# Experts in an order made on the chip, and S5's first tiles ahead of the convolution

## The chip, the cores and the metric

The kernel runs on one core of a Trainium2 chip. The core has TensorE (PE, matrix products into PSUM), VectorE (DVE), ScalarE (ACT), GpSimd (POOL) and SyncE (SP, which issues most DMAs here). Each engine works through its own instructions in order and waits on semaphores for the others. The metric is the device time in microseconds of one execution.

## The reference

A decoder trunk of two layers over 256 tokens of width 1024, all float32. Each layer has a mixer, a feed-forward part and a gated input embedding, each followed by a layer norm.

```
z = x @ w_in ; q, kv, gates, conv input, s5 input = split(z)
o_nsa  = attention: 8 query heads, 2 kv heads; compressed blocks (a small MLP over
         windows of 32 tokens), selected blocks and a sliding window, merged by gates
o_conv = GLU, causal depthwise convolution of width 31, layer norm, swish (256 channels)
o_s5   = 16 groups of 16 channels, each drives 64 complex states; scan over the tokens
x = LN(alpha * x + concat(o_nsa, o_conv, o_s5) @ w_out)
x = LN(alpha * x + ffn(x))     layer 0: dense SwiGLU, 2816 wide
                               layer 1: top 2 of 8 experts, SwiGLU, 3584 wide
x = LN(alpha * x + sigmoid(x Wg + bg) * (p @ Wp))
```

## The kernel before

The kernel is written with a tile framework: the program allocates tiles from pools (a tag has a number of buffers), the framework inserts the semaphores and orders each engine's instructions by program order and readiness as it reckons it when the program is built. `issue_after(i)` orders instructions of a block behind `i` on the same engine. Generators (`advance(gen, n)` runs n pieces) let the program interleave the parts of a mixer.

**The mixer** (`mixer`, once for each layer). With a PSUM pool of two double banks (`acc`) and four single banks (`tr`) it projects x: first the convolution's and S5's columns, then k and v with the convolution's replication pieces in between (`conv_taps`, tiles `rep` and `cu`), then q (tiles `qa`, two token halves). Then come, in program order: the rest of `conv_taps` (64 small matmuls for each of two channel halves, tile `cps`, with the taps from a 1 MiB load), the second piece of `compress` (four 1 MiB loads of `cmp_w1` and the hidden matmul `cmph`, L835, 64 entries in the trace), the rotary embedding of q (`rope`, tiles `rm` and `qr`), its transposes (`qTp`, L719) and those of k (`kTp`, copied by L728 and L729). All of these use the `tr` banks. Loads go through a ring of four `raw` buffers, so a load waits until the buffer four loads back is free.

Then `rest` opens a second PSUM pool (three banks `s`, one each of `o`, `y`, `bu`, two `tr`) and steps through the generators in an order written out by hand, `SEQ[l]`: `a` is one item of attention (scores L924 and L926, maximum L928, exponential L932, transposes L944, output L948), `s` one of S5's eight tiles (4 for each channel half), `c` a piece of the compressed branch, `v` the convolution's norm, `w` the splitting of a piece of w_out into high and low parts (L571, L573). An S5 tile (`s5_layer`, L1023 to L1047) is a pair of small matmuls into bank `bu` (L1026), two products with the table E on VectorE (L1031, L1032), a sum and a difference (L1033, L1034), two scans (L1038), a product for the real part (L1041, on VectorE or, for the tiles in `POOLA[l]`: 4 in layer 0, 0 to 4 in layer 1, on GpSimd), and one for the imaginary part on GpSimd (L1042). Its matmuls stand behind q's last matmul and its products behind the rotary embedding (`self.order`). At the end `advance(cmp)` finishes the compressed branch, whose transposed probabilities (L900) close attention's output of a token half (L952).

**The experts** (`moe`, layer 1). The router's counts come from a matmul; expert e gathers its tokens into 128 slots by one-hot matmuls (two experts share a gather, `pair`). `expert` streams 42 loads of 1 MiB (14 each of w1 and w3, in chunks of up to 1024 columns, then 14 of w2), issued by SyncE into a ring that in the end has 18 buffers. On TensorE each group of two loads is in an `If` on the expert's count:

```python
with self.tc.If(n > SM) as many:
    emit(False)
with many.Else():
    emit(True)
```

With at most SM = 64 tokens the two output halves go to two row halves of PSUM, with matmuls of 64 rows. Experts run in the order 0 to 7, with fixed addresses of their weights. Ahead of expert 1 stands `overflow`, for experts with over 128 tokens (a branch that jumps over it here). After the last expert come the projection and the gate of the input embedding.

Of the kernel before, what the change touches and what calls it, by code (L numbers as in the profile page):

```python
# [15 lines left out]
P = 128  # L16
D = 1024
S = 256
# [139 lines left out]

TORD = (1, 0)
ORDER = (4, 5, 0, 1, 2, 3, 6, 7)  # L160
SEQ = ("ascawcswwwwacwcwasasssaavsaswwwaaa", "accawwswcscawwsawsasasvsawaaswawaw")

POOLW = (0, 2, 4, 6)
POOLN = ((6, 7, 8, 9), (4, 9, 10, 11))
# [6 lines left out]
GRP = 2  # L171
SM = 64
OVF = 1
BK = 33

KCV = (1, 2)
# [28 lines left out]
class Trunk:  # L205
# [388 lines left out]
    def mixer(self, l, mp):  # L594
# [109 lines left out]
        for ku in range(2):  # L704
# [3 lines left out]
                    qlast = self.mm3(qa[tt], xh[:, k, tk(tt)], xl[:, k, tk(tt)], wh, wl, k == 0, k == 7)  # L708
            if ku == 0:
                advance(cmp, 1)  # L710
        advance(cv)
        advance(cmp, 1)
        qT = mp.tile([P, 4, S], F32, tag="qT", name="qT")
        for tt in range(TT):
            qr = mp.tile([P, 4, 2, 64], F32, tag="pT", name="qr", bufs=2)
            rlast = rope(qr.rearrange("p g v d -> p v g d"), qa[tt].rearrange("p (v g d) -> p v g d", v=2, g=4), tt, 2, 4)
            ps = self.tr("qTp")
            for g in range(4):
                nc.tensor.transpose(ps[:, g * P : (g + 1) * P], qr[:, g].rearrange("p v d -> p (v d)"), self.ident)  # L719
            qcopy = nc.scalar.activation(qT[:, :, tk(tt)], ps.rearrange("p (g t) -> p g t", g=4), AF.Copy, scale=0.125)  # L720


        ps = self.tr("kTp")
# [3 lines left out]
        p3 = ps.rearrange("p (b t) -> p b t", b=2)  # L727
        nc.scalar.activation(self.kTz[0:64, :, 0], p3[0:64], AF.Copy)  # L728
        nc.scalar.activation(self.kTz[64:128, :, 1], p3[64:128], AF.Copy)  # L729

        self.order = [qlast.ins, rlast.ins, qcopy]

        def rest():
            if l == 0:
# [59 lines left out]
    def compress(self, l, mp, flat, kr, vv, gt, qt):  # L794
# [28 lines left out]
                )  # L823
        yield

        ps = self.tr("cmph")
        ws = []
        for j in range(2):
            w1 = a["cmp_w1"][l, j].rearrange("(i p) f -> p i f", p=P)
            ws.append([self.load(w1[:, u * 8 : u * 8 + 8], 8, 256) for u in range(2)])  # L830
        for i in range(0, 16, 2):
            for j in range(2):
                for q in range(2):
                    r = (2 * j + q) * 32
                    mm(ps[r : r + 32, 0:256], flat[:, j, i + q].rearrange("p v n -> p (v n)"), ws[j][i // 8][:, i % 8 + q], start=(i == 0), stop=(i == 14))  # L835
# [173 lines left out]
    def s5_layer(self, l, mp, u5, mix):  # L1009
        nc = self.nc  # L1010
        col = self.col
        mag, CT, E = self.s5t
        mm = nc.tensor.matmul
        BT = col("BT", 512).rearrange("p (t k s) -> p t k s", t=2, k=2)
        glu = col("glu", 512).rearrange("p (k c) -> p k c", k=2)
        y = self.bank("y", "ya").rearrange("p (c t) -> p c t", c=2)
        self.new_xT(F32)
        for ct in range(2):
            hs = []
            for q in range(4):  # L1020
                j = 4 * ct + q
                r = slice(q * 32, q * 32 + 32)
                ps = self.bank("bu", "bu").rearrange("p (k t) -> p k t", k=2)  # L1023
                with self.tc.issue_after(self.order[0]):
                    for k in range(2):
                        mm(ps[:, k], BT[r, ct, k], u5[r, ct], start=True, stop=True)  # L1026
                eb = lambda k: E[:, k, j].unsqueeze(1).to_broadcast([P, 2, S])
                t1 = mp.tile([P, 2, S], F32, tag="s5t1", name="s5t1", bufs=2)
                t2 = mp.tile([P, 2, S], F32, tag="s5t2", name="s5t2", bufs=2)
                with self.tc.issue_after(self.order[1]):  # L1030
                    nc.vector.tensor_mul(t1, ps, eb(0))  # L1031
                    nc.vector.tensor_mul(t2, ps, eb(1))  # L1032
                nc.vector.tensor_add(t1[:, 0], t1[:, 0], t2[:, 1])  # L1033
                nc.vector.tensor_sub(t1[:, 1], t1[:, 1], t2[:, 0])  # L1034
                mb = mag[:, j : j + 1].to_broadcast([P, S])
                h = mp.tile([P, 2, S], F32, tag="s5h", name="s5h", bufs=2)
                for k in range(2):
                    nc.vector.tensor_tensor_scan(h[:, k], mb, t1[:, k], 0.0, op0=ALU.mult, op1=ALU.add)  # L1038

                ea, es = (t[:, 2 * q : 2 * q + 2] for t in (self.xh, self.xl))  # L1040
                (nc.gpsimd if j in POOLA[l] else nc.vector).tensor_tensor(ea, h, eb(0), op=ALU.mult)  # L1041
                nc.gpsimd.tensor_tensor(es, h, eb(1), op=ALU.mult)  # L1042

                hs.append(((0, ea[:, 0]), (1, es[:, 1]), (2, ea[:, 1]), (2, es[:, 0])))
                if q < 3:
                    yield

            for n in range(4):
                for q in range(4):
                    var, src = hs[q][n]  # L1050
                    mm(y[q * 32 : q * 32 + 32, ct], CT[:, var, 4 * ct + q], src, start=(n == 0), stop=(n == 3))
            yield
        z = u5
        for ct in range(2):
            nc.vector.scalar_tensor_tensor(z[:, ct], u5[:, ct], col("s5_d", 1, ct), y[:, ct], op0=ALU.mult, op1=ALU.add)
        t = mp.tile([P, 2, S], F32, tag="s5t2", name="s5g", bufs=2)
        self.gelu(t, z)
        nc.vector.scalar_tensor_tensor(z, t, 1.0, z, op0=ALU.add, op1=ALU.mult)
        ps = self.bank("bu", "glu").rearrange("p (c t) -> p c t", c=2)
        sg = mp.tile([P, 2, S], F32, tag="s5t1", name="s5sg", bufs=2)  # L1060
        for ct in range(2):
            for k in range(2):
                mm(ps[:, ct], glu[:, k, ct * P : (ct + 1) * P], z[:, k], start=(k == 0), stop=(k == 1))
            nc.scalar.activation(sg[:, ct], ps[:, ct], AF.Tanh, bias=col("s5_glu_b", 1, ct), scale=0.25)
        nc.vector.scalar_tensor_tensor(z, sg, 1.0, z, op0=ALU.add, op1=ALU.mult)
        sp = mp.tile([P, 4, S], F32R, tag="uz", name="sp")
        mix[6:8] = self.split_scaled(sp[:, 0:2], sp[:, 2:4], z, 0.25)
# [175 lines left out]
    def moe(self, l, mp):  # L1243
# [15 lines left out]
        def one_hot(e, tt):  # L1259
            Dm = Da[:, e // 2 % 2]  # L1260
            for i in range(2):
                self.dml = nc.vector.tensor_scalar(Dm[:, tt, i], slots, rank[:, tt, e + i : e + i + 1], sel[:, tt, e + i : e + i + 1], op0=ALU.is_equal, op1=ALU.mult)
            return Dm[:, tt].rearrange("p i s -> p (i s)")

        def split(tt):

# [50 lines left out]
            mm(ps[:, 0:NE], self.onesr, selr[:, tt], start=(tt == 0), stop=(tt == 1))  # L1317
        cnt = mp.tile([P, NE], F32, name="cnt")
        nc.vector.tensor_copy(cnt, ps[:, 0:NE])
        cint = mp.tile([1, 1 + NE], I32, name="cint")  # L1320
        nc.vector.tensor_copy(cint[:, 1:], cnt[0:1])
        advance(got)
# [4 lines left out]
        rank2 = mp.tile([P, TT, NE], F32, name="rank2")  # L1327
        nc.vector.tensor_scalar(cnt, cnt, float(SM), float(P - SM), op0=ALU.is_le, op1=ALU.mult)
        nc.vector.tensor_tensor(rank2, rank, cnt.unsqueeze(1).to_broadcast([P, TT, NE]), op=ALU.add)

        for tt in TORD:
            with self.after(lo):
# [10 lines left out]
            advance(self.gather(th, tl, [one_hot(e, tt) for tt in range(TT)], S, GT))  # L1343

        for e in range(NE):
            if e == OVF:

                self.flush()
                ov = self.over
                main = self.turned(ov[:2])  # L1350
                self.ring, self.nload = main, 0
                self.pre = [self.load(*s) for s in self.expert_loads(j, e)[: len(main)]]
                self.ring, self.nload = [ov] * ov[2], 0
                pre, self.pre = self.pre, []
                self.overflow(j, mp, Da[:, e // 2 % 2], cint, th, tl, rank, sel, comb, y)
                self.ring, self.pre, self.nload = main + self.ring, pre, len(main)
            Dm = Da[:, e // 2 % 2]
            es = ts(e % 2)
            De = [Dm[:, tt, e % 2] for tt in range(TT)]
            D2 = mp.tile([P, TT, P], F32, tag="D2", name="D2")  # L1360
            for tt in range(TT):
                nc.vector.tensor_scalar(D2[:, tt], slots, rank2[:, tt, e : e + 1], sel[:, tt, e : e + 1], op0=ALU.is_equal, op1=ALU.mult)
            ce = [comb[:, tt, e : e + 1] for tt in range(TT)]
            n = nc.tensor.value_load(cint[0:1, e + 1 : e + 2], min_val=0, max_val=S)
            ahead = (lambda: pair(e + 1)) if e % 2 and e + 1 != NE else None
            last = e == NE - 1
            self.expert(mp, self.expert_loads(j, e), n, self.xh[:, :, es], De, [D2[:, tt] for tt in range(TT)], ce, y, ahead, norm if last else None)
            if e == NE - 2:

                lnp = self.ln_params(l, 1, mp, "tl")  # L1370
                more = mp.tile([P, 2, D], F32R, tag="th", name="more")
                bias = self.ple_bias(l, mp.tile([P, D], F32, tag="h2", name="gb"), more[:, 0])
# [325 lines left out]
```

## Time and profile before

| what | us |
|---|---|
| median of 3 runs | 1585.9 |
| lowest and highest | 1584.85, 1587.26 |
| profiled execution, its own time | 1587.09 |
| span of its trace | 1585.3 |
| mixer, layer 0: from the first work to the attention stretch's end | 0 to 158 |
| dense layer, embedding | 185 to 420 |
| mixer, layer 1: attention stretch's end | 565 |
| experts 0 and 1 | 605 to 805 |
| experts 2 to 7 | 805 to 1534 |
| end | 1534 to 1585 |

Times of stages are from the span's start. A busy engine is not by itself the bound: in each stage one looks for the engine that is never idle, and for what the others waited for. Durations come from the one profiled execution.

### The profile page before, as it was taken

To read this page: it belongs to the slowest core of one execution; us is meant where nothing else is said; L and a number is where in the kernel's file an instruction comes from. 1 tells how busy PE (TensorE), PEld (TensorE's weight loads), DVE (VectorE), ACT (ScalarE), POOL (GpSimd) and SP (SyncE) were. 2 spreads that over 40 slices of the span, in tenths; PEclk is the share of its full clock that TensorE was granted. 3 is DMA by queue.
4 is the path that set the end of the run, shared out by engine and by line. 5 is a ranking of instruction groups with operands and counts; after the bars stand their busy time and mean duration, and the time that the engine had idled before them with its cause. 6 is when DMAs were issued, how large, how long until landed. Compare 5 with 4: busy or idle time off the path is not lost.

```text
span 1585.3 us, 16969 instructions
## 1 busy us (share of the span) xinstructions
PE 1468.0 (93%) x6654; PEld 835.4 (53%) x6655; DVE 600.4 (38%) x1023; ACT 368.6 (23%) x658; POOL 200.5 (13%) x162
## 2 busy tenths in 40 slices
PE   7987999999998798977999999999999999999887
PEld 6644788876775466422434644444644464343324
DVE  7479658646744955211211103211102110312224
ACT  5255555434444532100100001100000000101012
POOL 4625107502002511000000000000000000001000
PEclk9997999999999888999999999999999999999999
DMA  8341455553553049998999999999998889999991
GB/s 280 107 186 41 173 196 182 186 178 130 177 181 133 28 163 408 402 408 333 402 409 404 408 378 367 408 409 403 337 304 283 286 280 313 366 409 408 402 365 54
DMA packets 139916, 447.37 MB, mean 282 GB/s; under 512 B 7440, under 2 KB 19344, under 8 KB 138528
## 3 DMA queue, kind: packets, MB, share of 16 engines
q1 hardware_dynamic: 138784, 439.49, 74.6%
q0 software_dynamic: 1024, 6.35, 1.1%
q8 instruction: 79, 1.29, 0.3%
q14 instruction: 29, 0.24, 0.0%
HBM read 444.76 MB, written 1.05 MB: 281 GB/s over the span
## 4 chain that ended last, share of the span: by engine, by line
PE 45%; DMA 7%; DVE 1%; ACT 1%; issue 0%; SPq 0%; DVEq 0%; ACTq 0%
PE mgu L1476 27%; PE mo L1511 13%; DMA wraw<-in_moe_w_dram 7%; PE pg L587 2%; PE hT L1452 1%; PE xe L1401 1%; PE pp L1123 0%; PE sc L1531 0%; PE sc L1530 0%; PE DT L1494 0%; ACT ht L1457 0%; ACT hb L1483 0%; DVE mgu L1440 0%; SPq L261 0%; PE xtr L350 0%
## 5 line engine op out<-in xcount | busy, mean ns | idle before, releaser
L1476 PE MATMUL mgu<-wraw,xe 128*64 128x512 f32 (+3 forms) x2048 | 547.7, 545 | 31.4 <-DMA wraw<-in_moe_w_dram 17.8
L1476 PEld LDWEIGHTS mgu<-wraw,xe 128*64 128x64 f32 (+1 forms) x2048 | 247.5, 158 | 315.0 <-issue 269.6
L1511 PE MATMUL mo<-wraw,ht 128*64 128x512 f32 (+1 forms) x896 | 271.3, 595 | 10.2 <-DMA wraw<-in_moe_w_dram 10.2
L1511 PEld LDWEIGHTS mo<-wraw,ht 128*64 128x64 f32 (+1 forms) x896 | 101.4, 157 | 168.7 <-issue 144.1
L326 DVE TENSOR_TENSOR whl<-wraw,whl 128x1024 fp32r<-128x1024 f32 (+2 forms) x106 | 135.4, 1286 | 97.4 <-ACT whl L325 96.6
L325 ACT ACTIVATE whl<-wraw 128x1024 fp32r<-128x1024 f32 (+2 forms) x106 | 105.1, 997 | 114.6 <-PE fffn_w L322 44.6
L1484 DVE TENSOR_TENSOR hb<-hb,mgu 128x512 f32<-128x512 f32 (+1 forms) x64 | 38.1, 619 | 215.4 <-PE mgu L1476 215.1
L530 POOL DMA_DIRECT2D lnp<-in_lnp_dram x5 | 2.8, 567 | 834.8 <-ACT xe L1405 700.1
L1440 DVE MEMSET mgu<- 64x512 f32 x128 | 62.1, 485 | 118.8 <-ACT hb L1483 103.1
L1457 ACT ACTIVATE ht<-hT 128x512 f32<-128x512 f32 (+1 forms) x32 | 17.4, 544 | 371.7 <-PE hT L1452 354.6
L326 DVE TENSOR_TENSOR ot<-mo,ot 128x512 fp32r<-128x512 f32 x16 | 10.6, 688 | 240.0 <-ACT ot L325 240.0
L322 PE MATMUL fffn_w<-whl,xh 128*128 128x512 f32 (+1 forms) x192 | 71.8, 374 | 0.0
L321 PE MATMUL fffn_w<-whl,xl 128*128 128x512 f32 (+1 forms) x192 | 71.6, 373 | 0.0
L320 PE MATMUL fffn_w<-whl,xh 128*128 128x512 f32 (+1 forms) x192 | 71.6, 373 | 0.0
L1483 ACT ACTIVATE hb<-mgu 128x512 f32<-128x512 f32 (+1 forms) x64 | 32.4, 543 | 166.1 <-PE mgu L1476 163.0
L1455 DVE COPY ht<-hT 128x512 f32<-128x512 f32 (+1 forms) x32 | 20.0, 625 | 134.5 <-PE hT L1452 130.5
L325 ACT ACTIVATE ot<-mo 128x512 fp32r<-128x512 f32 x16 | 9.0, 596 | 263.7 <-PE mo L1511 263.7
L320 PEld LDWEIGHTS fffn_w<-whl,xh 128*128 128x128 f32 x192 | 36.1, 188 | 6.6
L321 PEld LDWEIGHTS fffn_w<-whl,xl 128*128 128x128 f32 x192 | 36.1, 188 | 6.5
L322 PEld LDWEIGHTS fffn_w<-whl,xh 128*128 128x128 f32 x192 | 36.1, 188 | 6.3
L1452 PEld LDWEIGHTS hT<-sqr,hb 128*128 128x128 f32 x224 | 24.8, 141 | 24.1 <-issue 18.5
L653 PE MATMUL z<-xh,whl 128*128 128x256 f32 x96 | 28.2, 294 | 8.4 <-ACT whl L325 8.4
(365 smaller groups left out, 1972.2 us busy)
## 6 DMA issues: line engine op xcount, KB each, us to landing
wraw<-in_moe_w_dram SPq DMA_DIRECT2D x336, 1024.0 KB, 16.4
wraw<-in_ffn_w_dram SPq DMA_DIRECT2D x33, 1024.0 KB, 5.1
wraw<-in_cmp_w_dram SPq DMA_DIRECT2D x8, 1024.0 KB, 5.5
wraw<-in_w_out_dram SPq DMA_DIRECT2D x8, 1024.0 KB, 10.9
wraw<-in_ple_gate_w_dram SPq DMA_DIRECT2D x8, 1024.0 KB, 10.7
wraw<-in_w_in_dram SPq DMA_DIRECT2D x8, 792.0 KB, 5.8
wraw<-in_w_in_dram SPq DMA_DIRECT2D x8, 768.0 KB, 7.5
lnp<-in_lnp_dram POOLq DMA_DIRECT2D x5, 1024.0 KB, 5.1
```

The source lines that it names most:

```text
L320: mm(dst, xh, wh, start=start, stop=False)
L321: mm(dst, xl, wh, start=False, stop=False)
L322: return mm(dst, xh, wl, start=False, stop=stop)
L325: h = self.hi = self.nc.scalar.activation(dh, src, AF.Copy)
L326: return h, (low or self.nc.vector).tensor_tensor(dl, src, dh.bitcast(F32), op=ALU.subtract)
L587: end = self.nc.tensor.matmul(at(acc, c), lh(k), parts[k][0][:, c], start=start, stop=stop)
L1440: nc.vector.memset(acc[h][rows[1 - h]], 0.0)
L1452: nc.tensor.transpose(ps[:, i * P : (i + 1) * P], hbs[h][:, i * P : (i + 1) * P], self.ident)
L1476: mm(dst, x, wk, start=k == 0, stop=k == KT - 1)
L1483: nc.scalar.activation(hb[:, :hw], accs[0][h][:, :hw], AF.Silu)
L1484: nc.vector.tensor_mul(hb[:, :hw], hb[:, :hw], accs[1][h][:, :hw])
L1511: mm(dst, x, w[:, i, h * 512 : (h + 1) * 512], start=k == 0, stop=k == NK - 1)
```

## The change

It has two parts. In both mixers, S5's first two tiles are issued ahead of the rest of `conv_taps`, with their matmuls in `tr` banks of the projection's pool; both rotary embeddings of q come ahead of them; the `y` bank is taken only after the first four tiles; `compress` has one more piece, so that its four loads stay where they were and its hidden matmul, now in a `tr` bank of the second pool, follows attention's first item (a `c` more in `SEQ`). In the experts, `take_turns`, ahead of expert 1, sorts experts 2 to 7 by their counts (ties by number) with VectorE, puts them into `TURNS` (position i gets the expert with the TURNS[i]-th largest count) and permutes the columns of ranks, selections, combination weights and counts; SyncE reads each turn's expert number into a register and forms the addresses of its 42 loads from it.

```diff
-SEQ = ("ascawcswwwwacwcwasasssaavsaswwwaaa", "accawwswcscawwsawsasasvsawaaswawaw")
+SEQ = ("acsacwcswwwwacwcwasasssaavsaswwwaaa", "acccawwswcscawwsawsasasvsawaaswawaw")
+FIX = 2
+TURNS = (0, 5, 1, 4, 3, 2)
...
-        advance(cv)
-        advance(cmp, 1)
         qT = mp.tile([P, 4, S], F32, tag="qT", name="qT")
+
+        qrs = []
         for tt in range(TT):
             qr = mp.tile([P, 4, 2, 64], F32, tag="pT", name="qr", bufs=2)
             rlast = rope(qr.rearrange("p g v d -> p v g d"), qa[tt].rearrange("p (v g d) -> p v g d", v=2, g=4), tt, 2, 4)
+            qrs.append(qr)
+        self.order = [qlast.ins, rlast.ins]
+        advance(s5, 2)
+        advance(cv)
+        advance(cmp, 1)
+        for tt in range(TT):
+            qr = qrs[tt]
             ps = self.tr("qTp")
...
-
-        self.order = [qlast.ins, rlast.ins, qcopy]
...
-        ps = self.tr("cmph")
         ws = []
         for j in range(2):
             w1 = a["cmp_w1"][l, j].rearrange("(i p) f -> p i f", p=P)
             ws.append([self.load(w1[:, u * 8 : u * 8 + 8], 8, 256) for u in range(2)])
+        yield
+        ps = self.tr("cmph")
...
-        y = self.bank("y", "ya").rearrange("p (c t) -> p c t", c=2)
+        y = None
...
-                ps = self.bank("bu", "bu").rearrange("p (k t) -> p k t", k=2)
+                ps = (self.tr("bu") if j < 2 else self.bank("bu", "bu")).rearrange("p (k t) -> p k t", k=2)
...
+            if y is None:
+                y = self.bank("y", "ya").rearrange("p (c t) -> p c t", c=2)
...
+        def column(name, e):
+
+            t, c = (tables[name], e) if e < FIX else (turned[name], e - FIX)
+            return [t[:, tt, c : c + 1] for tt in range(TT)]
+
+        def take_turns():
+
+            m = NE - FIX
+            key = mp.tile([P, NE], F32, name="tkey")
+            r = mp.tile([P, m], F32, name="trank")
+            one = mp.tile([P, m, m], F32, name="tone")
+            all = mp.tile([P, 4 * TT, m], F32, name="tall")
+            both = mp.tile([P, 4 * TT, m, m], F32, name="tboth")
+            got = mp.tile([P, 4 * TT, m], F32, name="tgot")
+            row = mp.tile([1, 2, m], I32, name="trow")
+            nc.vector.scalar_tensor_tensor(key, count, float(NE), slots[:, :NE], op0=ALU.mult, op1=ALU.subtract)
+            k = key[:, FIX:]
+            nc.vector.tensor_tensor(one, k.unsqueeze(1).to_broadcast([P, m, m]), k.unsqueeze(2).to_broadcast([P, m, m]), op=ALU.is_gt)
+            nc.vector.tensor_reduce(r, one, axis=AX.X, op=ALU.add)
+            for i, t in enumerate(TURNS):
+                nc.vector.tensor_scalar(one[:, i], r, float(t), None, op0=ALU.is_equal)
+            for i, t in enumerate((rank, sel, comb)):
+                nc.vector.tensor_copy(all[:, i * TT : (i + 1) * TT], t[:, :, FIX:])
+            nc.vector.tensor_copy(all[:, 3 * TT], count[:, FIX:])
+            nc.vector.tensor_copy(all[:, 3 * TT + 1], slots[:, FIX:NE])
+            wide = [P, 4 * TT, m, m]
+            nc.vector.tensor_tensor(both, all.unsqueeze(2).to_broadcast(wide), one.unsqueeze(1).to_broadcast(wide), op=ALU.mult)
+            nc.vector.tensor_reduce(got, both, axis=AX.X, op=ALU.add)
+            nc.vector.tensor_copy(row, got[0:1, 3 * TT :])
...
+            nc.vector.tensor_scalar(r, got[:, 3 * TT], float(SM), float(P - SM), op0=ALU.is_le, op1=ALU.mult)
+            nc.vector.tensor_tensor(turned["rank2"], turned["rank"], r.unsqueeze(1).to_broadcast([P, TT, m]), op=ALU.add)
+            return row
...
         for e in range(NE):
+            if e == 1:
+                row = take_turns()
             if e == OVF:
...
-            n = nc.tensor.value_load(cint[0:1, e + 1 : e + 2], min_val=0, max_val=S)
+            ce = column("comb", e)
+            which, own = e, cint[0:1, e + 1 : e + 2]
+            if e >= FIX:
+                own = row[0:1, 0, e - FIX : e - FIX + 1]
+                which = nc.sync.value_load(row[0:1, 1, e - FIX : e - FIX + 1], min_val=FIX, max_val=NE - 1)
+            n = nc.tensor.value_load(own, min_val=0, max_val=S)
...
-            self.expert(mp, self.expert_loads(j, e), n, self.xh[:, :, es], De, [D2[:, tt] for tt in range(TT)], ce, y, ahead, norm if last else None)
+            self.expert(mp, self.expert_loads(j, which), n, self.xh[:, :, es], De, [D2[:, tt] for tt in range(TT)], ce, y, ahead, norm if last else None)
```

## Rows read from the trace of the kernel before

**Rows 1.** The page's first part: busy us, share of the span, instructions.
```profile
PE 1468.0 (93%) x6654; PEld 835.4 (53%) x6655; DVE 600.4 (38%) x1023; ACT 368.6 (23%) x658; POOL 200.5 (13%) x162
```

**Rows 2.** Windows in both mixers: stretch, length, busy time by engine, clock, DMA.
```profile
74.00:88.00 14.00, 10.77 (x144) 6.88 (x137) 0.08 (x1) 3.48 (x7) 0.00 (x0) 1.00 0.60 222
88.00:158.00 70.00, 54.41 (x292) 31.47 (x291) 66.22 (x120) 38.65 (x100) 30.87 (x23) 0.83 0.23 84
...
481.70:497.00 15.30, 12.32 (x152) 7.53 (x145) 0.05 (x1) 4.43 (x8) 0.00 (x0) 0.89 0.62 223
497.00:565.00 68.00, 53.77 (x290) 30.64 (x289) 60.62 (x117) 38.97 (x107) 33.91 (x26) 0.82 0.15 55
```
The columns after the length are PE, PEld, DVE, ACT and POOL busy, the granted clock, the DMA share and GB/s.

**Rows 3.** Timeline of VectorE, both layers: start, us, instruction, idle before and releaser.
```profile
72.99 0.69 DVE L690 TENSOR_TENSOR qr<-rm,rm 128x512 f32<-128x512 f32 x1
87.92 0.69 DVE L928 TENSOR_REDUCE mx<-s 128x2 f32<-128x512 f32 x1 [14.24 <-PE s L926]
...
481.06 0.69 DVE L690 TENSOR_TENSOR qr<-rm,rm 128x512 f32<-128x512 f32 x1
497.11 0.69 DVE L928 TENSOR_REDUCE mx<-s 128x2 f32<-128x512 f32 x1 [15.35 <-PE s L926]
```

**Rows 4.** Timeline of TensorE: hidden matmul and first scores.
```profile
78.06 1.89 PE L835 MATMUL cmph<-wraw,flat 128*32 128x256 f32 x26
...
84.16 1.92 PE L835 MATMUL cmph<-wraw,flat 128*32 128x256 f32 x28 [2.75 <-DMA wraw<-in_cmp_w_dram]
86.56 1.12 PE L924 MATMUL s<-kTz,qT 128*128 128x512 f32 x2 [0.48 <-ACT chid L838]
...
495.32 1.56 PE L924 MATMUL s<-kTz,qT 128*128 128x512 f32 x2 [0.48 <-ACT chid L838]
```

**Rows 5.** Timeline of ScalarE: the last copy of k, both layers.
```profile
82.14 0.59 ACT L729 ACTIVATE kTz<-kTp 64x512 f32<-64x512 f32 x1
...
490.22 0.59 ACT L729 ACTIVATE kTz<-kTp 64x512 f32<-64x512 f32 x1
```

**Rows 6.** Windows for tile s5t alone: stretch, length, VectorE busy (instructions), clock, DMA.
```profile
88.00:158.00 70.00, 28.73 (x48) 0.83 0.23 84
497.00:565.00 68.00, 26.85 (x48) 0.82 0.15 55
```

**Rows 7.** Lines by form, layer 0 VectorE, then layer 1 GpSimd: S5's real part.
```profile
L1041 DVE TENSOR_TENSOR xh<-s5h,E 128x512 f32<-128x512 f32 x7 | 8.0, 1144 | 0.0
...
L1041 POOL TENSOR_TENSOR xh<-s5h,E 128x512 f32<-128x512 f32 x5 | 6.3, 1269 | 84.6 <-DVE s5h L1038 80.7 <-DVE su L933 3.8
```

**Rows 8.** Timeline of TensorE, layer 0: S5's matmuls, the compressed branch's end.
```profile
87.74 1.12 PE L1026 MATMUL bu<-u,pk 32*128 32x256 f32 x4
...
118.45 0.44 PE L900 MATMUL cpT<-sqr,pc 128*128 128x128 f32 x2
...
145.84 2.08 PE L952 MATMUL o<-pcT,VB 128*128 128x128 f32 x8
```

**Rows 9.** Windows by expert: experts 1, 4, 5, 6 and 7, as in group 2.
```profile
691.00:805.00 114.00, 90.60 (x440) 37.03 (x440) 23.51 (x46) 7.85 (x16) 0.00 (x0) 0.94 0.97 380
...
1042.00:1196.00 154.00, 152.83 (x419) 75.39 (x416) 21.68 (x40) 9.19 (x17) 0.00 (x0) 1.00 0.97 357
1196.00:1351.00 155.00, 153.64 (x440) 77.92 (x440) 21.73 (x40) 8.93 (x17) 0.60 (x1) 1.00 0.87 290
1351.00:1434.00 83.00, 81.03 (x412) 31.69 (x410) 20.11 (x38) 7.41 (x15) 1.95 (x3) 1.00 1.02 393
1434.00:1534.00 100.00, 84.80 (x406) 30.35 (x402) 18.89 (x34) 7.52 (x16) 3.40 (x2) 1.00 1.03 406
```

**Rows 10.** Timeline of VectorE: a small instruction of the router.
```profile
612.96 0.14 DVE L1328 TENSOR_SCALAR cnt<-cnt 128x8 f32<-128x8 f32 x1
```

**Rows 11.** The page's DMA issues: count, KB each, us from issue to landing.
```profile
wraw<-in_moe_w_dram SPq DMA_DIRECT2D x336, 1024.0 KB, 16.4
```

**Rows 12.** The chain that ended last: SyncE issuing one load.
```profile
734.25 0.52 SPq L261
```

More of the change, by code (lines that the diff above doesn't have):

```diff
@@ L719, in mixer @@
                 nc.tensor.transpose(ps[:, g * P : (g + 1) * P], qr[:, g].rearrange("p v d -> p (v d)"), self.ident)
[L720 removed]
+            nc.scalar.activation(qT[:, :, tk(tt)], ps.rearrange("p (g t) -> p g t", g=4), AF.Copy, scale=0.125)
         ps = self.tr("kTp")
@@ L1261, in one_hot @@
             for i in range(2):
-                self.dml = nc.vector.tensor_scalar(Dm[:, tt, i], slots, rank[:, tt, e + i : e + i + 1], sel[:, tt, e + i : e + i + 1], op0=ALU.is_equal, op1=ALU.mult)
+                r, s = (column(t, e + i)[tt] for t in ("rank", "sel"))
+                self.dml = nc.vector.tensor_scalar(Dm[:, tt, i], slots, r, s, op0=ALU.is_equal, op1=ALU.mult)
             return Dm[:, tt].rearrange("p i s -> p (i s)")
+        tables = {"rank": rank, "sel": sel, "comb": comb}
@@ new lines, in moe @@
+        turned = {}
+        def column(name, e):
[24 more added lines that the diff above has]
+            nc.vector.tensor_copy(row, got[0:1, 3 * TT :])
+            for i, n in enumerate(("rank", "sel", "comb")):
+                turned[n] = got[:, i * TT : (i + 1) * TT]
+            turned["rank2"] = mp.tile([P, TT, m], F32, name="trank2")
+            nc.vector.tensor_scalar(r, got[:, 3 * TT], float(SM), float(P - SM), op0=ALU.is_le, op1=ALU.mult)
+            nc.vector.tensor_tensor(turned["rank2"], turned["rank"], r.unsqueeze(1).to_broadcast([P, TT, m]), op=ALU.add)
+            return row
@@ L1319, in moe @@
         nc.vector.tensor_copy(cnt, ps[:, 0:NE])
+        count = mp.tile([P, NE], F32, name="count")
+        nc.vector.tensor_copy(count, cnt)
         cint = mp.tile([1, 1 + NE], I32, name="cint")
@@ L1329, in moe @@
         nc.vector.tensor_tensor(rank2, rank, cnt.unsqueeze(1).to_broadcast([P, TT, NE]), op=ALU.add)
+        tables["rank2"] = rank2
         for tt in TORD:
@@ L1361, in moe @@
             for tt in range(TT):
-                nc.vector.tensor_scalar(D2[:, tt], slots, rank2[:, tt, e : e + 1], sel[:, tt, e : e + 1], op0=ALU.is_equal, op1=ALU.mult)
-            ce = [comb[:, tt, e : e + 1] for tt in range(TT)]
-            n = nc.tensor.value_load(cint[0:1, e + 1 : e + 2], min_val=0, max_val=S)
+                nc.vector.tensor_scalar(D2[:, tt], slots, column("rank2", e)[tt], column("sel", e)[tt], op0=ALU.is_equal, op1=ALU.mult)
+            ce = column("comb", e)
[4 more added lines that the diff above has]
+            n = nc.tensor.value_load(own, min_val=0, max_val=S)
             ahead = (lambda: pair(e + 1)) if e % 2 and e + 1 != NE else None
             last = e == NE - 1
-            self.expert(mp, self.expert_loads(j, e), n, self.xh[:, :, es], De, [D2[:, tt] for tt in range(TT)], ce, y, ahead, norm if last else None)
+            self.expert(mp, self.expert_loads(j, which), n, self.xh[:, :, es], De, [D2[:, tt] for tt in range(TT)], ce, y, ahead, norm if last else None)
             if e == NE - 2:
```

## The prediction

> **What bounds the kernel now.** I read the page first. TensorE is busy for nearly all of the span and VectorE for little over a third [rows 1]; such averages hide stages with different limits, so I then asked for the busy time of each engine stage by stage. Only two kinds of stage are touched here.
>
> *The mixers.* In the long stretch of attention, S5 and convolution VectorE (DVE) is busy 66.2 of 70 us in layer 0 and 60.6 of 68 us in layer 1, while TensorE has 14 to 16 us of gaps [rows 2]: VectorE sets the end there. In the 14 to 15 us just before, VectorE does next to nothing [rows 2]. Its timeline shows why: it finishes the rotary embedding of q at 73.7 us and then has no work until attention's first scores at 87.9; in layer 1 it is 481.7 and 497.1 [rows 3]. TensorE's timeline shows what it waits for. The compressed branch's hidden matmul, begun among the convolution's matmuls, waits 2.75 us for its last weights; and the first scores come right behind the copy of that hidden tile out of PSUM, at 86.6 and 495.3 [rows 4], although q and k were in place at 82.7 and 490.8 [rows 5]. Two things to see: VectorE is idle in front of a stretch that it bounds, and that stretch opens about 4 us later than attention's own inputs would allow, held by the compressed branch.
>
> *The experts.* The stages of the trace show two kinds of expert. With more than 64 tokens ("many") one takes 154 to 155 us, PE busy throughout; with 64 or fewer ("few") 83 us, or 100 us where weights are late [rows 9]. Experts 2 to 7 are many, few, many, many, few, few by how long TensorE is busy in their stages (the stages of experts 2 and 3, 805 to 957 and 957 to 1042, repeat the two patterns and are not among the rows; experts 0 and 1 are few). Each has 42 loads of 1 MiB (336 of them for 8 experts, [rows 11]); at the 406 GB/s of the starved stage that is 2.58 us each and 108 us an expert. So a many expert lets the queue run ahead by some 46 us, a few expert uses up 25 us. The ring holds 18 buffers, so the lead can't pass 18 x 2.58 = 46 us: in the second of two many experts in a row the DMA share falls to 0.87 [rows 9].
>
> **The change, part by part.**
>
> *S5's first two tiles ahead of the convolution.* One tile on VectorE is six instructions on the s5t tiles plus the product for the real part. The six cost 28.73/8 = 3.59 us in layer 0 and 26.85/8 = 3.36 us in layer 1 [rows 6]; the product is 1.14 us on VectorE in layer 0 and is on GpSimd for these tiles in layer 1 [rows 7]. Two tiles are 9.5 and 6.7 us, together 16.2. They depend on u5, the table E and one small matmul pair each, ordered behind q's last matmul and the rotary embedding, so they may start at 73.7 and 481.7 and fit into the 14.2 and 15.4 us of idleness with 4.7 and 8.7 us to spare. In the old kernel they could not, since their PSUM bank belonged to the pool that opens when the projection's pool closes; the edit takes two of the projection's banks. Cost on TensorE: 1.1 us of matmuls a tile [rows 8], 2.2 us ahead of the convolution's last matmuls; the banks of q come free with the rotary embedding, which adds at most the 2 us by which that lags.
>
> *The compressed branch later.* Its hidden matmul now comes after attention's first item. Of its 64 entries in the trace 28 stood behind q and k; the other 36 stood in front, among the convolution's, and at 1.92/28 us each [rows 4] they give back 2.5 us. First scores then need only q and k: 82.7 + 2.2 - 2.5 = 82.4, so about 82.9 in place of 86.6 (3.7 us), and 491.0 in place of 495.3 (4.3 us). What gets late is the compressed result: its last transpose is at 118.5, its consumer, the close of attention's first output, at 145.8 [rows 8]. A delay of some 6 us of the branch lies inside those 27 us; without that cover it would cost the 6. In the same edit the weights' fourth load still waits for the taps' buffer; nothing of it is now waited for by the scores.
>
> *What of this reaches the end.* Bounds: 0, if every freed microsecond turns into another wait; 16.2 + 8.0 = 24.2, if VectorE stays as dense as it was. It will not quite, for the two tiles were filler between attention's dependent steps. Its idle share in the stretch is now 5% and 11% [rows 2]. I let it rise to 10% and 15%: layer 0 from 84.2 (the first maximum is 1.4 us behind the scores) with 66.2 - 9.5 = 56.7 us of work ends at 147.2 against 158, gain 10.8; layer 1 from 492.8 (1.8 behind) with 60.6 - 6.7 = 53.9 us ends at 556.2 against 565, gain 8.8. That is 19.6. Some 1.6 us are taken off for PSUM banks and for the hidden matmul in front of attention's second item: 18. All stages behind (the dense layer with TensorE full, and the expert loads, which start on events of the second mixer) begin earlier by the same amount.
>
> *The order of experts 2 to 7.* By counts, turns 0, 5, 1, 4, 3, 2 give many, few, many, few, few, many. Follow the lead of the loads. Both orders start the same: from 0 at expert 2 (stage 691 to 805 is bound by loads: TensorE idle 23 us at 380 GB/s [rows 9]), to about 46, down to 20, up to full again. Before: many (full, the queue is held up), then two few ones, which use 50 us against a lead of less than 46, some buffers being in use or in flight: 17 us of waiting (100 - 83) at the end. After: the two few ones stand right behind the same full ring, so they wait the same 17 us in the middle, and the many one last needs no lead. The sum is 3 x 154.5 + 3 x 83 + 17 = 730 us either way. I take 0 for the order, with bounds of -17 (the wait vanishes) and +17 (it comes twice).
>
> *Making it.* About 19 VectorE instructions, most as small as the 0.14 us one in [rows 10] and two of 288 columns: some 4 us. VectorE is busy 23.5 of 114 us in the stage of expert 1 and TensorE waits for weights there for longer than that; hidden, 0. Without that cover: 4 us. The six register reads on SyncE and the addresses made from a register are not in the trace. A plain load occupies the queue's issuer for 0.52 us out of the 2.58 us that its data take [rows 12]; below, 0; above, what a rival says. I take 0, nearest to that row.
>
> Sum: -18 - 0 - 0. The profiled execution took 1587.1 us (span 1585.3), 1.2 above the median of the runs, 1585.9; on the median the forecast is **1568 us**. A difference under 0.2% (3.2 us) can't be told from none here.
>
> **Rivals.**
>
> *The order pays too (0.07).* If the ring at the two few experts were fuller than I reckon, the wait of 17 us would be mostly gone: 1554. Against it: the same ring was full in front of them in the old order.
>
> *The freed time becomes other waits (0.12).* Attention's chain of scores, maximum, exponential, transposes may set the pace once S5 no longer fills its gaps; ScalarE is at half load, PE has gaps. Gain 0 to 6, about 1583; half of this lies within 0.2%. For it: 12 items that depend step by step. Against: VectorE's 5% idleness, which leaves no sign of waiting.
>
> *The tiles don't move (0.03).* If the two banks are not free until the rotary embedding is over and the convolution is served first, VectorE gets the work only when attention starts: 1585.
>
> *Register-addressed loads are slow (0.08, the other side).* Place: SyncE, 252 loads of experts 2 to 7. Of the two few experts' 84 loads, 66 must arrive while they run; with t us per load the time rises by 66 x (t - 2.58). At t = 2.85 this eats all 18 us; at t = 3.0 it is 28 us, 1596, slower than before. Against: a plain issue is 0.52 us, so an address would have to cost more than 2 us. [...]
>
> **How the numbers follow.** The forecast has 0.70, and its own range is 1559 to 1578. Faster by over 0.2%: 0.70 + 0.07 + 0.06 = 0.83. Within: 0.06 + 0.03 = 0.09. Slower: 0.08. The range 1556 to 1584 takes in the 24.2 us bound with some 5 us of it for the order, and most of the small gains; it leaves out the slow loads, the full 17 us of the order and the outer part of the forecast, some 0.18.
>
> **What would show it.** Right: VectorE busy with s5t instructions right after the rotary embedding in both layers; first scores about 4 us closer to the end of q; the VectorE-bound stretch ending about 11 and 9 us sooner; the last expert a many one without waits for weights, and 15 to 17 us of such waits in the two few ones before it; expert stages of 154 and 83 us. Wrong: s5t work still beside attention, a new gap in attention's first items on the hidden matmul, DMA share under 1 while TensorE waits for weights (slow loads), or no wait left in the few pair (the order pays).

## The result, and the profile after

The changed kernel takes 1568.1 us (median; 1566.98 to 1571.78), the kernel before 1585.94 on the same chip: ratio 0.9888, 95% interval 0.9876 to 0.9900. The profiled execution took 1566.98 us (span 1565.2) against 1587.09. The page's first part (answers to [rows 1]; VectorE's work is as before):

```profile
PE 1463.2 (93%) x6654; PEld 831.8 (53%) x6655; DVE 596.8 (38%) x1043; ACT 367.7 (23%) x658; POOL 200.0 (13%) x162
```

VectorE's timeline of layer 0 (columns as in [rows 3]): the first two S5 tiles fill 71.9 to 80.2 us, the first maximum comes at 81.23 in place of 87.92.

```profile
71.28 0.69 DVE L692 TENSOR_TENSOR qr<-rm,rm 128x512 f32<-128x512 f32 x1
71.89 0.68 DVE L1039 TENSOR_TENSOR s5t<-bu,E 128x512 f32<-128x512 f32 x1
...
79.49 0.69 DVE L1049 TENSOR_TENSOR xh<-s5h,E 128x512 f32<-128x512 f32 x1
81.23 0.69 DVE L936 TENSOR_REDUCE mx<-s 128x2 f32<-128x512 f32 x1 [1.05 <-PE s L934]
...
131.32 3.31 DVE L575 TENSOR_TENSOR wlo<-wraw,whi 128x512 fp32r<-128x512 f32 x2
134.56 1.74 DVE L1008 RECIPROCAL crs<-crs 128x256 f32<-128x256 f32 x1
136.22 2.18 DVE L575 TENSOR_TENSOR wlo<-wraw,whi 128x512 fp32r<-128x512 f32 x2
...
139.52 0.15 DVE L941 RECIPROCAL su<-su 128x2 f32<-128x2 f32 x1
139.60 0.67 DVE L936 TENSOR_REDUCE mx<-s 128x4 f32<-128x512 f32 x1
...
140.19 0.15 DVE L943 TENSOR_TENSOR su<-su,gt 128x2 f32<-128x2 f32 x1
```

TensorE's timeline (answers to [rows 4, 8]):

```profile
79.88 1.12 PE L932 MATMUL s<-kTz,qT 128*128 128x512 f32 x2 [1.34 <-ACT kTz L738]
...
87.56 1.05 PE L843 MATMUL cmph<-wraw,flat 128*32 128x256 f32 x10
88.54 0.66 PE L956 MATMUL o<-pT,vv 128*64 128x128 f32 x8
89.13 3.22 PE L843 MATMUL cmph<-wraw,flat 128*32 128x256 f32 x54
...
110.70 0.38 PE L908 MATMUL cpT<-sqr,pc 128*128 128x128 f32 x2
...
119.94 1.10 PE L999 MATMUL cmean<-cy,sqr 128*128 128x256 f32 x4
...
141.59 1.11 PE L952 MATMUL pT<-sqr,p 128*128 128x128 f32 x4 [9.20 <-POOL p L946]
...
145.84 0.71 PE L960 MATMUL o<-pcT,VB 128*128 128x128 f32 x4
```

The scores wait for k's copy alone; the hidden matmul stands behind them and no longer waits for a load. New is the wait of 9.2 us at 132 to 141. GpSimd is named, but it had to wait for VectorE in turn:

```profile
140.50 1.04 POOL L946 TENSOR_TENSOR p<-p,su 128x512 f32<-128x512 f32 x1 [3.26 <-DVE su L943]
```

It needs two VectorE instructions of 0.15 us on the item's sums (`su`). ScalarE had these sums ready at 126.3, but in VectorE's list above the two stand behind weight splits (`wlo`) and the convolution's norm.

The windows of the two stretches, from the first maximum to the first matmul of the output projection (answers to [rows 2]):

```profile
81.20:149.20 68.00, 54.20 (x347) 31.37 (x348) 55.08 (x108) 37.75 (x94) 27.23 (x22) 0.87 0.35 130
88.00:100.00 12.00, 12.00 (x140) 7.56 (x136) 6.69 (x20) 8.21 (x21) 2.81 (x2) 1.00 0.71 267
...
482.00:546.00 64.00, 53.15 (x340) 32.30 (x338) 52.25 (x105) 38.13 (x96) 26.74 (x22) 0.86 0.32 119
```

VectorE (DVE) has 11 us less work in layer 0 and 8 less in layer 1 (66.2 and 60.6 before; 9 less in layer 1 if the window of before, too, runs to that matmul, at 565.85), but is idle for 12.9 and 11.8 us. In 88 to 100 us TensorE is full and VectorE busy for 6.7 of 12.

The windows of experts 2 to 7 (answers to [rows 9]):

```profile
788.50:939.00 150.50, 150.07 (x408) 74.43 (x408) 21.16 (x40) 7.88 (x15) 0.00 (x0) 1.00 1.02 397
939.00:1027.00 88.00, 85.06 (x441) 37.06 (x440) 22.33 (x42) 8.93 (x19) 0.00 (x0) 1.00 1.02 395
1027.00:1178.60 151.60, 150.37 (x408) 74.42 (x408) 20.74 (x38) 8.05 (x16) 0.00 (x0) 1.00 0.97 354
1178.60:1266.50 87.90, 85.29 (x441) 35.32 (x440) 21.95 (x41) 9.01 (x19) 0.60 (x1) 1.00 1.02 395
1266.50:1363.50 97.00, 85.00 (x408) 31.11 (x408) 20.46 (x38) 7.64 (x16) 1.95 (x3) 1.00 1.03 406
1363.50:1514.00 150.50, 150.05 (x408) 74.45 (x408) 19.16 (x34) 7.87 (x15) 3.37 (x2) 1.00 0.80 316
```

Many, few, many, few, few, many; the second of the two few ones waits for weights at 406 GB/s, the last one for nothing. From TensorE's first instruction behind expert 1's last output matmul to its first behind the last expert's, the six take 725.7 us (788.47 to 1514.16) against 728.7 before (805.67 to 1534.35).

These 3 us have a visible source. The stages of the second and the fourth of the six have 33 matmuls more in the trace (441 against 408), 32 of them the gather of the next pair of experts. TensorE's groups in the fourth:

```profile
L1460 PE MATMUL xe<-Dm,th 128*128 128x256 f32 x16 | 4.2, 296 | 0.5 <-ACT hb L1542 0.5
...
L1460 PE MATMUL xe<-Dm,tl 128*128 128x256 f32 x16 | 3.9, 285 | 0.0
```

Before, the fourth was a many expert (x440 in [rows 9]), which took 155.8 us, 4.2 more than the many one ahead of it. Now it is the first of the two few ones, which wait for loads anyway: the two together take 184.9 us, against 183.7 before, and no many expert takes over 151.6.

So the profiled execution's 20.1 us are: 1.7 before the end of q's matmuls in layer 0 (the last section has their source), 8.0 and 8.2 in the mixers from there to the end of their output projections, 3.0 in experts 2 to 7, less 0.9 elsewhere.

### The profile page after: what moved, and what is told of

It is laid out like the page before. It is cut to its first block, busy times and chain, and to the rows that moved or that the text cites. A ratio compares the mean times of both kernels' runs of the same rounds, so it can differ in the third digit from the quotient of the medians.

```text
span 1565.2 us, 17518 instructions
## 1 busy us (share of the span) xinstructions
PE 1463.2 (93%) x6654; PEld 831.8 (53%) x6655; DVE 596.8 (38%) x1043; ACT 367.7 (23%) x658; POOL 200.0 (13%) x162
## 4 chain that ended last, share of the span: by engine, by line
PE 48%; DMA 4%; ACT 1%; SPq 1%; DVE 1%; issue 1%; ACTq 0%; DVEq 0%
PE mgu L1535 29%; PE mo L1570 13%; DMA wraw<-in_moe_w_dram 4%; PE pg L589 2%; PE hT L1511 1%; PE xe L1460 1%; SPq L263 1%; PE sc L1589 0%; PE sc L1590 0%; PE pp L1133 0%; PE DT L1553 0%; ACT ht L1516 0%; ACT hb L1542 0%; ACT ot L327 0%; DVE mgu L1499 0%
## 5 line engine op out<-in xcount | busy, mean ns | idle before, releaser
L328 DVE TENSOR_TENSOR ot<-mo,ot 128x512 fp32r<-128x512 f32 x16 | 10.6, 688 | 237.5 <-ACT ot L327 237.5
L324 PE MATMUL fffn_w<-whl,xh 128*128 128x512 f32 (+1 forms) x192 | 71.9, 374 | 0.0
```

What stands on the lines that cost most here:

```text
L324: return mm(dst, xh, wl, start=False, stop=stop)
L328: return h, (low or self.nc.vector).tensor_tensor(dl, src, dh.bitcast(F32), op=ALU.subtract)
```

## The experiments

Each experiment was timed in five rounds beside the kernel before. "Mixer 0" and "mixer 1" are the profiled time from the end of q's matmuls to the end of the output projection, less that of the kernel before (117.2 and 116.1 us); "experts" is that of experts 2 to 7, less 728.7. The six runs from "S5 ahead alone" to "two ahead, end as old" have the changed kernel's experts.

| run | median, us | ratio, 95% interval | mixer 0 | mixer 1 | experts |
|---|---|---|---|---|---|
| the changed kernel | 1568.1 | 0.9876 to 0.9900 | -8.0 | -8.2 | -3.0 |
| mixers alone | 1571.1 | 0.9885 to 0.9915 | -4.8 | -8.3 | -0.3 |
| order alone | 1584.89 | 0.9975 to 0.9993 | -0.2 | +1.0 | -2.2 |
| order made, old kinds | 1573.03 | 0.9891 to 0.9922 | -6.4 | -8.1 | +1.0 |
| alternating | 1554.23 | 0.9781 to 0.9808 | -6.7 | -8.1 | -16.0 |
| S5 ahead alone | 1568.71 | 0.9861 to 0.9896 | -9.3 | -6.2 | -1.4 |
| branch later alone | 1582.95 | 0.9963 to 0.9984 | -3.9 | -0.2 | -2.8 |
| one tile ahead | 1571.24 | 0.9884 to 0.9915 | -9.7 | -4.1 | -2.4 |
| three tiles ahead | 1585.25 | 0.9971 to 0.9998 | -1.5 | -1.1 | -1.5 |
| three ahead, end as changed | 1565.79 | 0.9843 to 0.9881 | -8.2 | -11.3 | -2.7 |
| two ahead, end as old | 1566.99 | 0.9849 to 0.9886 | -6.8 | -11.9 | -1.9 |
| alternating, one and three | 1550.66 | 0.9749 to 0.9790 | -7.5 | -11.5 | -15.9 |
| alternating, splits later | 1556.17 | 0.9783 to 0.9810 | -4.5 | -9.8 | -15.9 |

A mixer of the same program text varies by 3.3 us in these columns (mixer 0 of the changed kernel, mixers alone, order made, and alternating; mixer 1 by up to 1.7 with "splits later" taken in), so smaller differences in one of them prove nothing. In these four, TensorE, VectorE, ScalarE and GpSimd have their instructions of the stretch in the same order; TensorE's granted clock is not the same (1.00 or 0.83 over the same 10 us, last section).

**Mixers alone**: the experts stay 0 to 7 with fixed addresses.

```diff
-            if e == 1:
-                row = take_turns()
...
-            self.expert(mp, self.expert_loads(j, which), n, ...)
+            self.expert(mp, self.expert_loads(j, e), n, ...)
```

> Only the two mixers are changed; experts 2 to 7 run as numbered, with fixed addresses and nothing sorted. Theory (the mixers give the gain): the trace of the changed kernel is 17.2 us ahead of the old one where the experts begin, so 1569 us (1567 to 1571), ratio 0.989. Rival (the order gives the most of it): 1577 or more.

**Order alone**: the mixers of the kernel before (all mixer lines of the diff undone), experts as changed.

```diff
-        advance(s5, 2)
...
-        yield
-        ps = self.tr("cmph")
```

> Only the order of the experts is changed; the mixers are the old ones. Theory (the order moves the wait for weights of two few experts in a row from the end to the middle): no more than the 3 us by which the expert stage of the changed kernel is shorter, so 1583 to 1587. Rival (the order gives the most): 1577 or less.

**Order made, old kinds**: the order is made on the chip, and comes out as many, few, many, many, few, few.

```diff
-TURNS = (0, 5, 1, 4, 3, 2)
+TURNS = (0, 5, 1, 2, 4, 3)
```

> The whole change, but the turns are set so that kinds come as in the old order: many, few, many, many, few, few, still sorted on the chip and loaded from register addresses. Theory (making the order costs nothing): as the mixers alone, within 2 us. Rival (sorting, register reads or register addresses cost something that the order then repays): above the mixers alone by that price, 3 us or more.

**Alternating**: many, few, many, few, many, few.

```diff
-TURNS = (0, 5, 1, 4, 3, 2)
+TURNS = (0, 5, 1, 4, 2, 3)
```

> The whole change, but the last two turns change places: many, few, many, few, many, few. Theory (what waits is the second of two few experts in a row, 83 us of work against 108 us of loads, with a lead of at most 46 us): a many expert refills the lead before each few one, so the wait of about 16 us falls to 2 to 4 and the time to 1554 to 1558. Rival (the wait belongs to whatever comes last, or the lead is not refilled): 1566 or more.

These four ran on one chip, and each came out as its theory had it (mixers alone 0.1 us above its range). The mixers give 15.3 us, the order 1.5 by the medians, and making it, with addresses from registers, cannot be told from nothing (1573.03 against 1571.1, intervals nearly the same). Alternating gives 14 us more than the changed kernel. Its last three experts by windows:

```profile
1181.40:1269.30 87.90, 85.28 (x442) 35.37 (x441) 21.97 (x41) 9.04 (x18) 0.60 (x1) 1.00 1.02 395
1269.30:1420.70 151.40, 150.40 (x408) 74.40 (x408) 20.70 (x39) 7.92 (x15) 2.90 (x4) 1.00 0.98 361
1420.70:1503.90 83.20, 81.09 (x409) 31.41 (x408) 18.98 (x34) 7.80 (x16) 2.44 (x2) 1.00 1.00 388
```

The last few expert takes 83.2 us where the changed kernel's second few one took 97.0: the many one in front of it refilled the ring (361 GB/s over its 151.4 us are 54.7 MB, 10.6 more than the 42 loads of one expert).

**S5 ahead alone**: the hidden matmul goes back ahead of the first scores.

```diff
-SEQ = ("acsacwcswwwwacwcwasasssaavsaswwwaaa", "acccawwswcscawwsawsasasvsawaaswawaw")
+SEQ = ("ascawcswwwwacwcwasasssaavsaswwwaaa", "accawwswcscawwsawsasasvsawaaswawaw")
...
+        ps = self.tr("cmph")
         ws = []
...
-        yield
-        ps = self.tr("cmph")
```

> The changed kernel with the compressed branch's hidden matmul put back among the convolution's matmuls, ahead of attention's first scores; S5's two tiles stay ahead, the experts' order stays the new one. Theory (two separate gifts: 16 us of tile work taken out of the VectorE-bound stretch, and an earlier start of that stretch): only the tile work is kept; first scores are held again by the hidden tile, so 7 to 9 us of the two mixers' gain go back and the time is 1575 to 1578. Rival (one gift: the stretch starts earlier only because VectorE and TensorE are kept busy ahead of it, the place of the hidden matmul is nothing): 1568 to 1571.

**Branch later alone**: no S5 tile ahead.

```diff
-        advance(s5, 2)
...
-                ps = (self.tr("bu") if j < 2 else self.bank("bu", "bu")).rearrange("p (k t) -> p k t", k=2)
+                ps = self.bank("bu", "bu").rearrange("p (k t) -> p k t", k=2)
```

> The changed kernel without S5's two tiles ahead of the convolution (S5 takes its first tiles beside attention, as the old kernel did); the hidden matmul stays behind attention's first item. Theory of two separate gifts: first scores come 4 to 5 us closer to the end of q in each layer and the stretch still holds all of S5's work, so some 8 us of the 15 are kept: 1574 to 1578. Rival (with S5 in it the stretch is bound by VectorE's work from the end of the rotary embedding on, so that an earlier score only queues up): 1582 to 1584.

The first theory fell in both, and both times lie in the rival's range: S5 ahead alone is as fast as the whole change, the branch alone gives 4.3 us (2.5 to 5.9), and in its profile 2.3 us stand before the end of q (the clock, 1.00 in place of 0.60 from 22 to 26 us, last section, and a wait of TensorE for VectorE ahead of it, 0.6 us in place of 1.6). TensorE's timeline and the stretches' windows of S5 ahead alone:

```profile
83.86 3.49 PE L842 MATMUL cmph<-wraw,flat 128*32 128x256 f32 x28 [2.61 <-DMA wraw<-in_cmp_w_dram]
87.83 1.12 PE L931 MATMUL s<-kTz,qT 128*128 128x512 f32 x2 [0.48 <-ACT chid L845]
```

```profile
89.20:145.00 55.80, 49.06 (x276) 28.89 (x275) 53.72 (x103) 35.67 (x83) 27.34 (x20) 0.88 0.23 86
...
485.50:545.70 60.20, 48.41 (x276) 30.11 (x274) 57.74 (x105) 36.77 (x95) 25.42 (x20) 0.82 0.25 88
```

The scores come 8 us later than in the changed kernel, and the output projection begins 4.3 us earlier (144.96 against 149.24; it ends 0.8 earlier, at 177.06): VectorE is busy for 53.7 of 55.8 us, where the changed kernel needs 68.0 for 55.1. The windows of branch later alone say the same:

```profile
79.60:152.00 72.40, 58.73 (x355) 33.07 (x356) 66.73 (x120) 39.36 (x101) 31.33 (x23) 0.83 0.31 115
485.90:561.60 75.70, 61.10 (x359) 34.59 (x358) 62.45 (x120) 40.58 (x110) 33.82 (x26) 0.80 0.23 82
```

The stretches begin earlier and get longer (from 70 and, up to the same matmul, 69 us) with the same work in them to within 1 us. The start of the scores is not what sets their end.

**One tile ahead** (`advance(s5, 1)`, one `tr` bank) and **three tiles ahead** (`advance(s5, 3)`, three banks):

```diff
-        advance(s5, 2)
+        advance(s5, 1)
...
-                ps = (self.tr("bu") if j < 2 else ...
+                ps = (self.tr("bu") if j < 1 else ...
```

> One S5 tile ahead of the convolution in each layer in place of two. Theory (each tile is worth its VectorE time, 4.8 us in layer 0 and 3.4 in layer 1): 8 us slower than the changed kernel, 1574 to 1577. Rival (the first tile fills the idle time and the second only takes its place in the queue ahead of the copies that the scores need): 1568 to 1571, as the changed kernel.

> Three S5 tiles ahead of the convolution in each layer in place of two. VectorE has 0.7 to 1.2 us left between the second tile and the first maximum in layer 0. Theory (the idle time is used up; a third tile delays the first maxima by what it takes off later): within 3 us of the changed kernel, 1565 to 1571, the first maximum of layer 0 some 4 us later. Rival (attention's steps, not VectorE's work, set the pace behind, so a third tile still pays its own time): 1560 to 1564.

One tile took 1571.24 us, just above the rival's range and below the theory's. In layer 1 the gain grows with the tiles: 0.2, 4.1 and 8.2 us with none, one and two. In layer 0 the first tile already pays all (3.9, 9.7 and 8.0). Three tiles came out as neither theory had it: nearly all is lost. TensorE's timeline of that run:

```profile
137.48 2.08 PE L1073 MATMUL glu<-u,pk 128*128 128x256 f32 x4 [7.29 <-DVE u L1068]
...
143.63 1.03 PE L999 MATMUL cmean<-cy,sqr 128*128 128x256 f32 x4
...
156.11 1.22 PE L322 MATMUL wo<-whi,ch 128*128 128x512 f32 x2 [2.75 <-ACT ch L332]
```

`SEQ` counts steps: with three tiles taken ahead, each later `s` does the next tile, and S5's end (`glu`) falls ahead of the `v` of the convolution's norm. TensorE waits 7.3 us for S5's end, the convolution's mean behind it in its queue comes at 143.6 in place of 119.9, and the output projection, which begins with the convolution (`ch`), at 156. The next two runs took steps out of `SEQ`:

```diff
 three ahead, end as changed (besides advance(s5, 3)):
-SEQ = ("acsacwcswwww...", "acccawwswcsc...")
+SEQ = ("acacwcswwww...", "acccawwwcsc...")
 two ahead, end as old:
+SEQ = ("acacwcwwww...", "acccawwwccaww...")
```

> Three S5 tiles ahead, and one step of S5 taken out of the hand-written order of each mixer, so that the fourth and later tiles and S5's end stand where the changed kernel has them. Theory (the run with three tiles lost 17 us because every later step of S5 moved up one place, so that S5's end stood ahead of the convolution's normalization on the same PSUM banks and engines, and TensorE waited 7.3 us for it): the loss goes, 1563 to 1570. Rival (a third tile costs attention's first items more than it takes off later, wherever the others stand): 1577 to 1587.

> Two S5 tiles ahead as in the changed kernel, and two steps of S5 taken out of the hand-written order of each mixer, so that the other six tiles and S5's end stand where the old kernel had them. Theory (what pays is two tiles' work less in the stretch that VectorE bounds): as the changed kernel, 1565 to 1571. Rival (what pays is that all later steps of S5, its end above all, came two places earlier in the order): most of the gain goes, 1578 to 1585.

Both theories held: the loss goes, so it came from the places of S5's later steps, and the gain of two tiles does not come from these places. In layer 1 two tiles with S5's end at its old place give as much (11.9) as three (11.3), so the third is not what pays there; in layer 0 neither gains over one tile.

**Alternating, one and three**, and **alternating, splits later**:

```diff
 one and three (besides the turns of alternating, and one s less in layer 1's SEQ):
+AHEAD = (1, 3)
-        advance(s5, 2)
+        advance(s5, AHEAD[l])
 splits later (besides the turns of alternating), the end of layer 0's SEQ:
-...asssaavsaswwwaaa
+...asssaavsasawawaw
```

> The alternating order of experts (many, few, many, few, many, few), with one S5 tile ahead in layer 0 and three in layer 1 (one later step of S5 taken out of layer 1's order, so that S5's end stands there where the changed kernel has it). Theory (the two layers add up, each as it was in the runs that tried it alone: layer 0 some 1.7 us and layer 1 some 3 us better than with two tiles, both counted from the end of q): 5 us faster than the run with the alternating order alone, 1547 to 1551. Rival (these differences come from how the build arranges each whole program and don't carry over): 1552 to 1558.

> The alternating order of experts, the mixers as in the changed kernel but for the end of layer 0's order: the last three weight splits stand between attention's last three items and no longer ahead of them. Theory (TensorE's 9.2 us wait near 140 us is VectorE's: the maximum of attention's next item is queued behind the weight splits, so with the splits later it goes first): the wait goes and layer 0's output projection ends 3 to 7 us sooner, 1547 to 1551. Rival (the output projection needs the split weights right behind, so the wait only changes its place): 1552 to 1556, with TensorE waiting for the split weights.

The first is the fastest kernel of the study by its median, 1550.66 us, though its interval overlaps that of alternating alone. Layer 1's gain carried over (-11.5). Layer 0 gives -7.5 in place of -9.7, 0.8 better than the two tiles of alternating (-6.7); that is inside the scatter, so this half of the theory is not shown. In the second the rival held, 0.2 us above its range: the wait only changed its place, to S5's end though, and not to the split weights as I had it. Its waits of TensorE, 66 to 165 us (total, times, longest), then those of the run with the alternating order alone:

```profile
PE glu L1073 <- DVE u L1068: 6.4, 1, 6.4
PE pT L952 <- POOL p L946: 4.7, 3, 2.3
```

```profile
PE pT L952 <- POOL p L946: 11.6, 3, 9.2
```

VectorE has to do the same work there, whichever consumer waits for it. The theory also had the wrong instruction: not the next item's maximum, but the waiting item's own two `su` instructions came behind the splits.

## Why the prediction was right, and where it was not

- **S5's tiles, 9.5 and 6.7 us.** Right in size for two: alone they give 9.3 and 6.2, with S5's end at its old place 6.8 and 11.9. As a price for each tile it fails in layer 0, where one gives 9.7 (5.9 more than none) and a second and third nothing more.
- **First scores 3.7 and 4.3 us earlier.** They came 5.0 and 5.7 earlier, counted from the end of q; the mechanism was right, the size a little low. The compressed result came earlier and not later: its last transpose is at 110.7 (118.45 before), its consumer at 145.84 as before, so the cover held, with more room than reckoned.
- **What of this reaches the end: the step that failed.** I let VectorE's idle share rise to 10% and 15%, which left 3.4 of the 8 us of earlier scores standing (19.6 less the tiles' 16.2), and took off 1.6 for PSUM banks and the hidden matmul. The share rose to 19% and 18% (12.9 of 68.0, 11.8 of 64.0), and beside the tiles the earlier scores are worth nothing that the runs can tell: without them the time is the same. So the rival that freed time becomes other waits was true of the scores and not of the tiles. Where it went is seen in part only. TensorE is full from 80 to 100 us (busy for 20.00 of 20) with the hidden matmul and S5's matmuls, while VectorE idles 5.3 of 12 us (0.4 in the kernel before). The new wait of 9.2 us is not the place: VectorE is busy without a gap from 130 to 140 (10.00 of 10), and taking it away in "splits later" gained nothing.
- **18 us for the mixers** came out as 16.2 in them, 1.7 ahead of the end of q that I had not foreseen, and 3 in the experts (less 0.9 elsewhere). That the time is that of the forecast is in part luck: these made up for one another. The medians are 17.8 apart.
- **The order, 0.** It is 1.5 us alone by the medians (1.1 to 4.0 by its interval). The wait for weights moved from the end to the second of the two few experts, as followed from the ring's lead; it is 13.8 us there (97.0 less 83.2) and was reckoned 17. What the sum over "either way" left out is the gather of the next pair: it took 4.2 us in a many expert and now lies where loads are waited for. All eight profiles with this order are 1.4 to 3.0 us shorter in the experts, the two with the old kinds 0.3 shorter and 1.0 longer. So the stages are not 154 and 83 us, but 151 and, with the gather, 88. The bound of -17 is what the alternating order reaches (-16.0).
- **Making the order, and register addresses, 0.** VectorE makes it at 599 to 602 us, beside expert 0's matmuls, in 2.8 us where 4 were reckoned: the rows below. The new instructions of SyncE, from its instructions at the loads' line (minimum, median and longest ns), add 46 and 29 ns to a load; the rival needed 270 to eat 18 us. The loads of the starved stage ran at 406 GB/s, as before, so no cost of SyncE's new instructions shows there.

```profile
599.15 0.15 DVE L1294 SCALAR_TENSOR_TENSOR tkey<-count,sqr 128x8 f32<-128x8 f32 x1
...
601.75 0.15 DVE L1312 TENSOR_TENSOR trank<-tgot,trank 128x12 f32<-128x12 f32 x1
```

```profile
L263 SPq FUSED_REGOPS  x252: 42/46/56, 770.5 to 1450.0; - x126
L263 SPq MOVE wraw<-in_moe_w_dram x252: 29/29/38, 770.6 to 1450.2; - x126
```

What stays open: why one tile suffices in layer 0. With one tile in place of two each engine has its instructions in another order over most of the stretch, and no run held that order fixed.

## What to carry to other kernels

Work taken out of a stretch that one engine bounds was worth about its time here (two tiles, reckoned at 9.5 and 6.7 us, gave 9.3 and 6.2), though in layer 0 the first tile gave all of it. Opening that stretch earlier was worth nothing beside it (1568.1 against 1568.71 us); the same busy time over more microseconds shows this (VectorE 66.7 over 72.4 in place of 66.2 over 70). In an order written out by hand that counts steps, moving one step ahead moves every later one: look whether it has to come out of the list too, or a consumer far behind may be late, as the output projection was here (156 us in place of 149). Where loads run ahead into a ring, as here, it paid to put a stage that lets them lead in front of each one that uses up the lead (83.2 us in place of 97.0), and other work (here the gather, 4.2 us) where the loads are waited for.

## What the runs showed of the hardware that was not expected

TensorE's granted clock near the start differs between kernels whose program text there is the same. Windows of the kernel before, then of the changed kernel, then of two ahead, end as old:

```profile
18.00:22.00 4.00, 2.25 (x16) 1.85 (x15) 3.90 (x12) 3.18 (x8) 0.00 (x0) 0.97 0.90 349
22.00:26.00 4.00, 4.00 (x24) 4.00 (x23) 3.57 (x9) 0.86 (x1) 0.00 (x0) 0.60 0.84 219
```

```profile
18.00:22.00 4.00, 2.40 (x19) 2.04 (x18) 3.86 (x12) 3.52 (x9) 0.00 (x0) 1.00 0.92 356
22.00:26.00 4.00, 4.00 (x37) 4.00 (x37) 4.00 (x12) 1.79 (x3) 0.00 (x0) 1.00 0.74 209
```

```profile
18.00:22.00 4.00, 1.98 (x14) 1.58 (x14) 3.86 (x12) 3.71 (x9) 0.00 (x0) 1.00 0.96 373
22.00:26.00 4.00, 4.00 (x23) 4.00 (x22) 3.39 (x7) 0.86 (x1) 0.00 (x0) 0.57 0.66 190
```

TensorE waits in the first window in all three (busy 2.25, 2.40 and 1.98 of 4.00 us). Behind it the granted clock is 0.60 in the first and 0.57 in the third, and 24 and 23 matmuls go through in 4 us in place of 37 at 1.00; by my estimate the 13 fewer of the first, at 4.00/37 us each, are 1.4 of the 1.7 us by which q ended earlier in the changed kernel. Of the fourteen kernels only these two and "order alone" have a clock under 1.00 there (0.60, 0.57 and 0.59), and in these three q's matmuls end at 70.4 to 71.1 us, in the others at 68.1 to 69.3. They are also the ones in which TensorE waited twice there, 1.6 us for VectorE and 0.2 to 0.4 for ScalarE. "Two ahead, end as old" has the new mixers, so it is not the change as such; what decides it stays open.

The clock also differs between mixers of the same text. From 10 to 20 us behind the end of q's matmuls in layer 0 TensorE waits 1.3 us for k's copy in the changed kernel and in alternating alike; the windows, in this order:

```profile
78.68:88.68 10.00, 8.80 (x39) 4.17 (x41) 8.55 (x19) 4.98 (x16) 3.04 (x2) 1.00 0.84 315
```

```profile
78.78:88.78 10.00, 8.79 (x24) 3.84 (x25) 7.22 (x16) 3.97 (x13) 3.04 (x2) 0.83 0.85 315
```

"Mixers alone" and "order made" have 0.83 there too, so the changed kernel's mixer 0 (-8.0 against -4.8 to -6.7) had the better clock there, 1.00. At the same clock one tile remains no worse than two: -9.7 and -8.0 at 1.00, -7.5 and -6.7 at 0.83 (the two alternating runs).
